# A decoder layer on one core: the queries' scale moved into constants, two Z projections moved into the attention steps, and the last stage's VectorE order written by hand

## The chip, the cores and the metric

The kernel runs on one core of a Trainium2 chip. The core has five engines, each with its own instruction queue that is worked off in order: TensorE (PE, matmuls), VectorE (DVE), ScalarE (ACT), GpSimd (POOL) and SyncE (SP, which here only issues DMA transfers). They meet through semaphores. On-chip data lie in SBUF, results of TensorE in PSUM banks. The metric is the device time of one execution in microseconds; the median over the runs counts.

## The reference

One decoder layer on 1024 tokens of width 1024, in float32, and a last norm:

```python
h = rmsnorm(x, attn_norm_w[l])
proj = h @ w_in[l]
qkv_la, z_la, b_la, a_la, q_d, k_d, v_d = jnp.split(proj, SPLIT_IDX, axis=-1)
qkv_la = jax.nn.silu(causal_conv(qkv_la, conv_w[l]))
...
o_la = gated_delta_rule(q_la, k_la, v_la, g, beta)        # q = l2norm(q) * DK ** -0.5
o_la = rmsnorm(o_la, la_norm_w[l]) * jax.nn.silu(z_la.reshape(B, T, LA_HEADS, LA_DV))
...
o_d = diff_attention(q_d, k_d, v_d, lam, rel_bias)        # p = softmax_0 - lam * softmax_1
o_d = rmsnorm(o_d, diff_norm_w[l], eps=1e-5) * (1.0 - lam_init)
x = x + jnp.concatenate([o_la, o_d], axis=-1) @ w_out[l]
h = rmsnorm(x, ffn_norm_w[l])
gate, up = jnp.split(h @ w_gate_up[l], 2, axis=-1)
x = x + (jax.nn.silu(gate) * up) @ w_down[l]
return rmsnorm(x, final_norm_w)
```

The delta rule and the attention have four heads each (head widths 128). The delta rule's output is normalized per token and head (`rmsnorm`), so a constant factor on its queries matters only against the norm's epsilon.

## The kernel before

**Matmuls.** A float32 product is computed as three products of a reduced type: each operand is split into a high part (a cast) and a low part (the difference), and `mm3` (L147 to L150) adds high x high, high x low and low x high. `split` makes the parts of a weight: the cast on ScalarE (L155), the difference on VectorE (L157, one instruction) or GpSimd (L161, two halves). A projection of one head (`dense_T`, `qk_dense`) is 48 matmuls of 512 columns: 2 halves of the tokens x 8 x 3.

**Stages.** 1. Norm of the input, its transposed high and low parts `xT_h`, `xT_l`, and the convolved projections of the delta rule. 2. The chunks' products: `brk`, `dec`, `At` and the intra-chunk matrix (L513, L516; L520 copies the diagonal blocks), norms of keys and queries by `pow` on GpSimd (`nk` L526, `rqs` L527), and the inverses of the triangular blocks on VectorE (L538 to L545), while TensorE runs the attention's query and key projections of heads 0 and 1 (`qk_dense`; results evacuated by ScalarE at L569 and L570, and stored to DRAM as `qh`, `ql`, `ks`). `TT` (written at L618) holds the transposed inverses. 3. The recurrence over 8 chunks of 128 tokens, whose outputs `Vn` are scaled by `oms` (L739 to L743), and around it the four Z projections (L745 to L749): a `dense_T` each, `Silu` on ScalarE, a store to `sz_dr`. 4. The attention: 32 steps (4 heads x 8 query blocks). A step k has its score matmuls (`emit_S`, L963 and L964), the maximum on VectorE (L969 to L974), the exponentials on ScalarE (L978), the difference of the two maps (`emit_P`, L987 to L990), and, one and two steps later, its transposes (`emit_T`, L1005, copied at L1006) and its values (`emit_PV`, L1020). After every fourth step comes a norm of four blocks (L1027 to L1035, with a `pow` on GpSimd at L1032), and `emit_OT`. 5. The residual, the second norm and the feed-forward network. 6. The last stage: for each row block t the last two rows of the down projection are added (`add`, L1248, two halves), then the final norm (L1555 to L1568) and the output's store.

**Fillers.** TensorE would wait in an attention step for the chain through VectorE and ScalarE. A generator `fill()` (L843) hands out other matmuls: before, the query and key projections of heads 2 and 3, the gate of the delta rule's heads, and the output projection of the delta rule's heads. `pump(n)` takes about n matmuls from it, and `share(k)` (L922) says how many step k takes.

**Pools.** `cv` and `avl` are rotating buffers of four tiles of 128x1024 each: a fifth request waits until the first tile's last reader is done.

**Order.** In stage 4 SyncE's order is that of the code (`manual_schedule`). Everywhere else a scheduler, at build time, sets the order of each engine's queue; so an instruction can stand far ahead of where the code has it. L660 stands in the code after the inverses, in VectorE's queue before them.

Of the kernel before, what the change touches and what calls it, by code (L numbers as in the profile page):

```python
# [8 lines left out]
F32 = mybir.dt.float32  # L9
# [61 lines left out]
def decoder_kernel(ctx: ExitStack, tc: tile.TileContext, a: dict, out: bass.AP):  # L71
# [479 lines left out]
    def qk_dense(h, is_q, ps_of, mid=None):  # L551
        if (h, is_q) not in raws:
            fetch((h, is_q), *qk_col(h, is_q))
        w = take((h, is_q), nc.gpsimd if h > 1 else None)
        yield 0
        sh = cvt(F32R)
        sl = cvt(F32R)
        for n in range(2):
            if n and mid:
                mid()  # L560
            ps = ps_of(n)
            wh, wl = w
            ns = slice(n * 512, (n + 1) * 512)
            for k in range(NK):
                mm3(ps, wh[:, k, :], wl[:, k, :], xT_h[:, k, ns], xT_l[:, k, ns], k == 0, k == NK - 1)
                yield 3
            scale = DH ** -0.5 if is_q else 1.0
            if h < 2:
                nc.scalar.mul(out=sh[:, ns], in_=ps, mul=scale)  # L569
                nc.scalar.mul(out=sl[:, ns].bitcast(F32), in_=ps, mul=scale)  # L570
                if n == 1:
                    nc.vector.tensor_tensor(out=sl, in0=sl.bitcast(F32), in1=sh.bitcast(F32), op=ALU.subtract)
                continue
            nc.scalar.mul(out=sl[:, ns].bitcast(F32), in_=ps, mul=scale)
            nc.scalar.copy(out=sh[:, ns], in_=sl[:, ns].bitcast(F32))
            nc.gpsimd.tensor_tensor(out=sl[:, ns], in0=sl[:, ns].bitcast(F32), in1=sh[:, ns].bitcast(F32),
                                    op=ALU.subtract)
        if is_q:
            nc.scalar.dma_start(out=qh_dr[h], in_=sh.bitcast(F32))
            nc.scalar.dma_start(out=ql_dr[h], in_=sl.bitcast(F32))  # L580
        else:
            nc.scalar.dma_start(out=ks_dr[h].rearrange("(a d) t -> a d t", d=DH)[0::3], in_=sh.bitcast(F32))
            nc.scalar.dma_start(out=ks_dr[h][DH:3 * DH, :], in_=sl.bitcast(F32))
# [69 lines left out]
    for h in range(H):  # L653
        ut = sm()
        for j in range(NT):
# [1 line left out]
                             start=True, stop=True)  # L657
        nc.vector.tensor_scalar(out=TT[h][0:64, :, 64:128], in0=ut[0:64].rearrange("p (j c) -> p j c", c=64),
                                scalar1=-1.0, scalar2=None, op0=ALU.mult)
    nc.vector.tensor_scalar(out=rqs, in0=rqs, scalar1=DK ** -0.5, scalar2=None, op0=ALU.mult)  # L660
    Ktok = gp.tile([P, NHJ, P], F32, name="ak", bufs=1)
    for h in range(H):
        Kh = Ktok[:, h * 8:h * 8 + 8, :]
# [74 lines left out]
    rq = rqs.rearrange(fl)  # L738
    nc.vector.tensor_tensor(out=oms, in0=oms, in1=rq, op=ALU.mult)  # L739
    nc.vector.tensor_tensor(out=oms, in0=oms, in1=rq, op=ALU.mult)  # L740
    nc.vector.tensor_scalar(out=oms, in0=oms, scalar1=1.0 / DV, scalar2=1e-6, op0=ALU.mult, op1=ALU.add)
    nc.gpsimd.tensor_tensor(out=oms, in0=oms, in1=epow_neg, op=ALU.pow)
    nc.vector.tensor_tensor(out=oms, in0=oms, in1=rq, op=ALU.mult)  # L743

    for h in range(H):  # L745
        zps = dense_T(C_Z + h * P, nc.vector)
        sz = cvt()
        nc.scalar.activation(out=sz, in_=zps, func=AF.Silu)
        nc.scalar.dma_start(out=sz_dr[h], in_=sz)  # L749
# [89 lines left out]
    def x2_load(t):  # L839
        x2t[t] = op.tile([P, T], F32, name="avl", bufs=4)  # L840
        nc.sync.dma_start(out=x2t[t], in_=x2_dr[t])

    def fill():  # L843
        one = lambda n: flr()
        yield from qk_dense(2, True, one, lambda: finish_norm(0))
        fetch((3, True), *qk_col(3, True))
        finish_norm(1)
# [74 lines left out]
    def share(k):  # L922
        i = steps[k][1] if k < len(steps) else 0
        prev = steps[k - 1][1] if 0 < k <= len(steps) else 0
        n = 22 - 5 * i / 2
        pb = 4 if prev >= 4 else 0
        return max(0, n - pb - 5), pb, 5

# [129 lines left out]
            nc.scalar.dma_start(out=md[h][:, hc], in_=m)  # L1058

    with tc.manual_schedule(engines={mybir.EngineType.SP}):  # L1060
        fetch((2, True), *qk_col(2, True))
        fetch((2, False), *qk_col(2, False))
        load_head(0)
        load_v(0)
        for k in range(len(steps) + 4):

            def values():
                if 2 <= k < len(steps) + 2:
                    emit_PV(k - 2)

            if k < len(steps):
                emit_S(k, values)
                if k % NT == 0:
                    load_q(k // NT, 1 - first_half(k // NT))
                if k % NT == 4 and k // NT + 1 < H:
                    load_head(k // NT + 1)
                    load_v(k // NT + 1)
            else:
                values()
            if k == 28:  # L1080
                late["mix"][1] = [cvt(F32R) for h in range(H)]
                load_mix_d(1, H - 1)
            pa, pb, pc = share(k)
            pump(pa)
            if 1 <= k <= len(steps):
                emit_T(k - 1, pb)
            pump(pc)
            if k > 2 and (k - 3) % 4 == 3:
                emit_OT(k - 3)
            if k < len(steps):  # L1090
                emit_P(k)
            if k == len(steps):
                while 0 not in late["mix"]:
                    pump(12)
                load_mix_d(0, H - 1)
        while "d1" in late:
            c = next(filler, None)
            if c is None:
                break
# [446 lines left out]
                add(x2[:, i + 4, n0], x2[:, i + 4, n0], mid[:, i, :])  # L1546
                add(x2[:, i + 4, n1], x2[:, i + 4, n1], mid[:, i, :])

    for t in range(NT):
        ssn = small.tile([P, 2], F32, name="ssn", bufs=3)  # L1550
        for n in range(2):
            ns = slice(n * 512, (n + 1) * 512)
            add(x2[:, t, ns], plain(t, n, (NF - 2, NF - 1)), x2[:, t, ns])
            sc = cvt()
            nc.scalar.activation(out=sc[:, ns], in_=x2[:, t, ns], func=AF.Square, accum_out=ssn[:, n:n + 1])  # L1555
        nc.vector.tensor_tensor(out=ssn[:, 0:1], in0=ssn[:, 0:1], in1=ssn[:, 1:2], op=ALU.add)
        nc.vector.tensor_scalar(out=ssn[:, 0:1], in0=ssn[:, 0:1], scalar1=1.0 / D, scalar2=1e-6,
                                op0=ALU.mult, op1=ALU.add)
        nc.gpsimd.tensor_tensor(out=ssn[:, 1:2], in0=ssn[:, 0:1], in1=epow_neg[:, 0:1], op=ALU.pow)
        o = cvt()  # L1560
        for n in range(2):
            ns = slice(n * 512, (n + 1) * 512)
            if n == 0 and t < NT - 1:
                nc.scalar.activation(out=o[:, ns], in_=x2[:, t, ns], func=AF.Copy, scale=ssn[:, 1:2])
                nc.gpsimd.tensor_tensor(out=o[:, ns], in0=o[:, ns], in1=wb3[:, ns], op=ALU.mult)
            else:
                nc.vector.scalar_tensor_tensor(out=o[:, ns], in0=x2[:, t, ns], scalar=ssn[:, 1:2],
                                               in1=wb3[:, ns], op0=ALU.mult, op1=ALU.mult)  # L1568
            nc.sync.dma_start(out=out[0, t * P:(t + 1) * P, ns], in_=o[:, ns])
    close_ep()  # L1570
    late["close_wp2"]()
    late["close_x2"]()
# [32 lines left out]
```

## Time and profile before

| | us |
|---|---|
| runs | 1336.72, 1341.82, 1337.94 |
| median | 1337.94 |
| profiled execution: its own time | 1337.53 |
| its span on the core | 1335.8 |
| TensorE busy | 1267.1 (95%) |
| VectorE busy | 835.5 (63%) |
| ScalarE busy | 530.2 (40%) |
| GpSimd busy | 293.9 (22%) |

The span runs from the first to the last instruction; 1.7 us of the execution's time lie outside it. Busy times are sums over instructions. [...] In a timeline the bracket at a row's end is the engine's idle time before it and what ended it; rows of equal instructions are drawn together (x4).

### The profile page before, as it was taken

The page shows a single profiled execution, that of the slowest core. Times are in us where ns is not written, and L with a number is a line of the kernel's source. Part 1 is how long each engine was busy: PE and PEld are TensorE (multiplying, and loading weights), DVE is VectorE, ACT ScalarE, POOL GpSimd, SP SyncE. Part 2 cuts the span into 40 slices and gives each one's busy share as a digit, 9 for nine tenths or more (in the row PEclk, how much of TensorE's full clock was granted, in tenths as well). Part 3 has the DMA queues.
Part 4 walks back from the last instruction along what each step waited for, and adds up shares of the span by engine and source line. Part 5 has one row for each costly group of instructions (what it writes and reads, how often), then busy time and mean ns, then how long its engine had stood idle before and what let it go on. Part 6 is the DMA issues. An engine that isn't in the chain of part 4 may idle for free.

```text
span 1335.8 us, 17311 instructions
## 1 busy us (share of the span) xinstructions
PE 1267.1 (95%) x6432; PEld 1059.9 (79%) x6432; DVE 835.5 (63%) x1383; ACT 530.2 (40%) x1030; POOL 293.9 (22%) x231
## 2 busy tenths in 40 slices
PE   6999988999999998998979999999999999999996
PEld 6978876798988776887758888888888888778775
DVE  6515756833853776776786556565566536687876
ACT  5224342222544654554553333233323317243314
POOL 1014443200013432113222222212212110121104
PEclk9999998999999998999989999999999999999998
DMA  7425662410026656643512343333323346676503
GB/s 220 115 63 205 221 221 80 136 37 17 18 74 198 200 174 197 229 151 134 177 61 95 119 123 110 106 118 115 113 90 116 103 158 238 204 237 205 188 2 126
DMA packets 143884, 183.44 MB, mean 137 GB/s; under 512 B 15888, under 2 KB 92984, under 8 KB 143800
## 3 DMA queue, kind: packets, MB, share of 16 engines
q1 hardware_dynamic: 135888, 168.19, 39.3%
q10 hardware_dynamic: 7912, 14.16, 2.9%
q8 instruction: 50, 0.82, 0.3%
q14 instruction: 34, 0.28, 0.1%
HBM read 127.00 MB, written 55.32 MB: 136 GB/s over the span
## 4 chain that ended last, share of the span: by engine, by line
PE 62%; DVE 12%; ACT 3%; issue 3%; POOL 3%; DMA 3%; POOLq 0%; DVEq 0%; ACTq 0%
PE big L1236 17%; PE sm L1236 8%; PE big L1535 5%; PE fl L1236 4%; PE fl L1535 3%; PE sm L1535 3%; PE big L148 2%; PE big L149 2%; PE big L150 2%; PE fl L148 2%; PE fl L150 2%; PE fl L149 2%; PE sm L1020 1%; DVE mx L969 1%; DMA ks<-cv 1%
## 5 line engine op out<-in xcount | busy, mean ns | idle before, releaser
L148 PE MATMUL big<-xT_h,w_h 128*128 128x512 f32 x320 | 128.2, 401 | 6.1 <-ACT cv L570 5.7
L150 PE MATMUL big<-xT_h,w_l 128*128 128x512 f32 x320 | 126.8, 397 | 2.0 <-DVE w_l L157 2.0
L149 PE MATMUL big<-xT_l,w_h 128*128 128x512 f32 x320 | 126.5, 395 | 0.0
L1248 DVE TENSOR_TENSOR av<-big,av 128x512 f32<-128x512 f32 x79 | 54.3, 688 | 59.2 <-PE big L1236 59.1
L1236 PE MATMUL big<-hT_h,cv 128*128 128x512 f32 x264 | 85.9, 389 | 0.0
L1236 PE MATMUL big<-hT_h,avl 128*128 128x512 f32 x264 | 85.9, 389 | 0.0
L148 PEld LDWEIGHTS big<-xT_h,w_h 128*128 128x128 f32 x320 | 60.8, 190 | 21.2 <-ACT cv L570 7.6
L150 PEld LDWEIGHTS big<-xT_h,w_l 128*128 128x128 f32 x320 | 60.7, 190 | 15.3 <-DVE w_l L157 2.8
L149 PEld LDWEIGHTS big<-xT_l,w_h 128*128 128x128 f32 x320 | 60.8, 190 | 12.0 <-issue 0.2
L155 ACT CAST w_h<-w_raw 128x1024 fp32r<-128x1024 f32 x32 | 33.5, 1051 | 83.8 <-PE big L149 66.5
L161 POOL TENSOR_TENSOR w_l<-w_raw,w_h 128x512 fp32r<-128x512 f32 x28 | 38.2, 1383 | 117.5 <-ACT w_h L155 116.3
L1141 POOL TENSOR_TENSOR avl<-xh,avl 128x512 fp32r<-128x512 f32 x23 | 33.1, 1440 | 138.2 <-ACT avl L1140 138.2
L454 POOL TENSOR_TENSOR avl<-avl 128x512 f32<-128x512 f32 x36 | 49.1, 1363 | 60.1 <-DMA avl<-in_w_down 25.2
L1236 PE MATMUL sm<-hB_h,avl 128*128 128x512 f32 x176 | 59.3, 399 | 1.1 <-ACT hB_h L1166 1.1
L1141 POOL TENSOR_TENSOR cv<-xh,cv 128x512 fp32r<-128x512 f32 x22 | 30.7, 1396 | 132.6 <-ACT cv L1140 132.6
L978 ACT ACTIVATE ae<-big,mx 128x128 f32<-128x128 f32 (+7 forms) x64 | 47.3, 741 | 27.9 <-DVE mx L969 11.9
L1236 PE MATMUL sm<-hB_h,cv 128*128 128x512 f32 x176 | 57.8, 389 | 0.0
L1236 PEld LDWEIGHTS big<-hT_h,avl 128*128 128x128 f32 x264 | 49.6, 188 | 10.3
L1236 PEld LDWEIGHTS big<-hT_h,cv 128*128 128x128 f32 x264 | 49.6, 188 | 10.3
L157 DVE TENSOR_TENSOR w_l<-w_raw,w_h 128x1024 fp32r<-128x1024 f32 x18 | 23.3, 1295 | 52.7 <-ACT w_h L155 35.8
L1513 POOL TENSOR_TENSOR x<-x,w_raw 128x512 f32<-128x512 f32 x16 | 22.0, 1383 | 155.4 <-DVE x L1248 122.7
L1204 DVE TENSOR_TENSOR xh<-w_raw 128x512 f32<-128x512 f32 x45 | 31.6, 701 | 33.9 <-DMA w_raw<-in_w_gate_up 33.9
(451 smaller groups left out, 3627.2 us busy)
## 6 DMA issues: line engine op xcount, KB each, us to landing
w_raw<-in_w_gate_up SPq DMA_DIRECT2D x44, 512.0 KB, 4.0
w_raw<-in_w_in SPq DMA_DIRECT2D x24, 512.0 KB, 4.7
sum<-av SPq DMA_DIRECT2D x45, 256.0 KB, 3.0
avl<-in_w_down SPq DMA_DIRECT2D x18, 512.0 KB, 5.3
rows<-avl SPq DMA_DIRECT2D x18, 512.0 KB, 2.8
w_raw<-sum SPq DMA_DIRECT2D x11, 512.0 KB, 3.5
xh<-sum SPq DMA_DIRECT2D x21, 256.0 KB, 3.9
av<-sum SPq DMA_DIRECT2D x10, 512.0 KB, 3.7
```

The lines of the kernel that those rows point to most:

```text
L148: nc.tensor.matmul(ps, lhsT=lh, rhs=rh, start=start, stop=False)
L149: nc.tensor.matmul(ps, lhsT=lh, rhs=rl, start=False, stop=False)
L150: nc.tensor.matmul(ps, lhsT=ll, rhs=rh, start=False, stop=stop)
L155: nc.scalar.copy(out=h, in_=raw)
L161: eng.tensor_tensor(out=l[:, c], in0=raw[:, c], in1=h[:, c].bitcast(F32), op=ALU.subtract)
L454: nc.gpsimd.tensor_tensor(out=o, in0=x, in1=y, op=ALU.subtract)
L978: nc.scalar.activation(out=e[:, :n].rearrange("p (b c) -> p b c", b=nb), in_=s[:, :, :w], func=AF.Exp, bias=mx[:, m:m + 1], accum_out=zs[: ...
L1141: eng.tensor_tensor(out=l, in0=raw, in1=h.bitcast(F32), op=ALU.subtract)
L1204: nc.vector.tensor_tensor(out=r, in0=a0, in1=a1, op=alu)
L1236: nc.tensor.matmul(ps, lhsT=x[:, k, :], rhs=y[:, k, :], start=begin and k == 0 and n == 0, stop=k == HALF - 1 and n == 2, skip_group_check ...
L1248: nc.vector.tensor_tensor(out=out, in0=in0, in1=in1, op=ALU.add)
L1535: nc.tensor.matmul(pss[i], lhsT=x[:, g_, ts], rhs=y[:, g_, :], start=begin and g_ == 0 and n_ == 0, stop=g_ == GRP - 1 and n_ == 2, skip_g ...
```

## The change

It has four parts.

1. `rqs`, the reciprocal norms of the delta rule's queries, is no longer multiplied by `DK ** -0.5` (L660). The factor goes into two constants where `oms` is made.
2. In `qk_dense` the low part `sl` comes from the pool of `avl` instead of `cv`, but for the last key projection.
3. The Z projections of heads 2 and 3 leave the loop behind the recurrence and become the first two fillers (`z_dense`), with their weights' low parts on GpSimd instead of VectorE and the `Silu` in two halves. `share` hands out 24.67 - 2.5 i instead of 22 - 2.5 i, and SyncE fetches their weights first.
4. The last stage is cut into `final_sum`, `final_norm` and `final_out`, and VectorE's order there is that of the code.

```diff
-        sl = cvt(F32R)
+        sl = cvt(F32R) if (h, is_q) == (H - 1, False) else opt("avl", F32R)
...
-    nc.vector.tensor_scalar(out=rqs, in0=rqs, scalar1=DK ** -0.5, scalar2=None, op0=ALU.mult)
...
-    nc.vector.tensor_scalar(out=oms, in0=oms, scalar1=1.0 / DV, scalar2=1e-6, op0=ALU.mult, op1=ALU.add)
+    nc.vector.tensor_scalar(out=oms, in0=oms, scalar1=1.0 / (DK * DV), scalar2=1e-6, op0=ALU.mult, op1=ALU.add)
     nc.gpsimd.tensor_tensor(out=oms, in0=oms, in1=epow_neg, op=ALU.pow)
-    nc.vector.tensor_tensor(out=oms, in0=oms, in1=rq, op=ALU.mult)
-
-    for h in range(H):
+    nc.vector.scalar_tensor_tensor(out=oms, in0=oms, scalar=DK ** -0.5, in1=rq, op0=ALU.mult, op1=ALU.mult)
+
+    for h in range(2):
         zps = dense_T(C_Z + h * P, nc.vector)
...
+    def z_dense(h):
+        w = take(("z", h), nc.gpsimd)
+        fetch((2, h == 2), *qk_col(2, h == 2))
+        sz = cvt()
+        for n in range(2):
+            ps = flr()
+            ns = slice(n * 512, (n + 1) * 512)
+            for k in range(NK):
+                mm3(ps, w[0][:, k, :], w[1][:, k, :], xT_h[:, k, ns], xT_l[:, k, ns], k == 0, k == NK - 1)
+                yield 3
+            nc.scalar.activation(out=sz[:, ns], in_=ps, func=AF.Silu)
+        nc.scalar.dma_start(out=sz_dr[h], in_=sz)
...
     def fill():
         one = lambda n: flr()
+        yield from z_dense(2)
+        yield from z_dense(3)
         yield from qk_dense(2, True, one, lambda: finish_norm(0))
...
-        n = 22 - 5 * i / 2
+        n = 24.67 - 5 * i / 2
...
-        fetch((2, True), *qk_col(2, True))
-        fetch((2, False), *qk_col(2, False))
+        for h in (2, 3):
+            fetch(("z", h), w_in_v[:, :, C_Z + h * P:C_Z + (h + 1) * P], [P, NK, P])
...
+    with tc.manual_schedule(engines={mybir.EngineType.DVE}):
+        final_sum(0, 0)
+        final_sum(0, 1)
+        for t in range(NT):
+            if t + 1 < NT:
+                final_sum(t + 1, 0)
+            ssn = final_norm(t)
+            if t + 1 < NT:
+                final_sum(t + 1, 1)
+            final_out(t, ssn)
```

VectorE in stage 2, where L660 stood: one piece of the difference (`ak` are the chunks' products, read from PSUM; `rqs` comes from GpSimd's `pow`).

```order
 L501 TENSOR_SCALAR ssq<-ssq 128x8
 L513 SCALAR_TENSOR_TENSOR ak<-fl,brk,dec 128x128 x4
-L660 TENSOR_SCALAR rqs<-rqs 128x32
 L516 TENSOR_TENSOR dec<-sm,dec 128x512
 L513 SCALAR_TENSOR_TENSOR ak<-fl,brk,dec 128x128 x4
```

The row between the two groups of L513 is gone; all else there keeps its order.

ScalarE at the start of the attention, of the kernel before and then of the change (L978 before and L992 now are the exponentials, L852 the `Silu` of a half Z projection, L1006 and L1020 copies of the transposes).

```order
L978 ACT_TABLE_LOAD
L978 ACTIVATE ae,z<-big,mx 128x128 x2
L574 ACTIVATE cv<-fl 128x512
L575 CAST cv<-cv 128x512
L978 ACTIVATE ae,z<-big,mx 128x256 x2
L1006 COPY apt<-sm 128x128
```

```order
L852 ACTIVATE cv<-fl 128x512
L992 ACT_TABLE_LOAD
L992 ACTIVATE ae,z<-big,mx 128x128 x2
L992 ACTIVATE ae,z<-big,mx 128x256 x2
L1020 COPY apt<-sm 128x128
L852 ACT_TABLE_LOAD
L852 ACTIVATE cv<-fl 128x512
L1036 ACTIVATE aon<-sm,rz 128x128
L853 DMA sz_79<-cv 128x1024
L992 ACT_TABLE_LOAD
L992 ACTIVATE ae,z<-big,mx 128x384 x2
```

Each switch from an exponential to a `Silu` and back has a table load; there are seven in the attention now, and one before.

VectorE in the last stage, one row block of the kernel before and then of the change (L1248 and L1262 are the sums, first half from `fl`, second from `sm`; L1567 and L1590 the products that make the output).

```order
L1248 TENSOR_TENSOR x_9138<-fl,x_9138 128x512
L1556 TENSOR_TENSOR ssn<-ssn 128x1
L1557 TENSOR_SCALAR ssn<-ssn 128x1
L1567 SCALAR_TENSOR_TENSOR cv<-x_9138,ssn,wb_9132 128x512
L1248 TENSOR_TENSOR x_9138<-sm,x_9138 128x512
```

```order
L1262 TENSOR_TENSOR x_9143<-fl,x_9143 128x512
L1576 TENSOR_TENSOR ssn<-ssn 128x1
L1577 TENSOR_SCALAR ssn<-ssn 128x1
L1262 TENSOR_TENSOR x_9143<-sm,x_9143 128x512
L1590 SCALAR_TENSOR_TENSOR cv<-x_9143,ssn,wb_9137 128x512
```

The second sum of the next block now stands between the norm's scalars and the product that waits for GpSimd's `pow`.

Two more things come out of the new order. On GpSimd the last norm but one of the attention (L1032 before, L1046 now) stood behind one of four halves of a weight split and stands ahead of all four. And the dense matmuls (three to a k block) that TensorE has ahead of the second score block, then in each attention step, counted from its queue, are:

| | before | after |
|---|---|---|
| behind the recurrence, up to the attention's first blocks | 128 | 54 |
| steps 0 to 7 | 24, 18, 18, 12, 0, 24, 0, 15 | 5, 21, 21, 15, 15, 21, 4, 8 |
| steps 8 to 15 | 21, 12, 21, 3, 0, 24, 11, 6 | 24, 12, 0, 24, 33, 12, 3, 21 |
| steps 16 to 23 | 7, 0, 24, 36, 12, 9, 9, 9 | 3, 0, 24, 19, 5, 0, 30, 9 |
| steps 24 to 30 | 9, 9, 9, 12, 15, 15, 0 | 9, 12, 12, 15, 15, 21, 21 |
| last reader of `xT` at the end of step | 13 | 18 |

## Rows read from the trace of the kernel before

**Rows 1.** The page, part 1: busy time, share of the span, instructions.

```profile
PE 1267.1 (95%) x6432; PEld 1059.9 (79%) x6432; DVE 835.5 (63%) x1383; ACT 530.2 (40%) x1030; POOL 293.9 (22%) x231
```

**Rows 2.** Windows: stretch, length, busy time by engine, mean clock, DMA share.

```profile
core 0: us, PE busy (x) PEld busy (x) DVE busy (x) ACT busy (x) POOL busy (x), PEclk, DMA share, GB/s
210.00:230.00 20.00, 13.53 (x45) 9.68 (x45) 16.78 (x40) 4.46 (x10) 1.60 (x1) 0.74 0.23 79
414.00:640.00 226.00, 209.37 (x1158) 175.58 (x1157) 156.75 (x284) 121.16 (x273) 63.30 (x51) 0.98 0.55 177
510.00:530.00 20.00, 15.48 (x81) 13.55 (x81) 11.02 (x22) 8.99 (x24) 2.87 (x3) 0.83 0.69 216
610.00:620.00 10.00, 6.19 (x27) 5.19 (x27) 7.49 (x17) 3.26 (x11) 2.46 (x2) 0.83 0.72 243
```

**Rows 3.** Timeline of VectorE, 201 to 212: start, duration, instruction, idle before.

```profile
201.68 1.13 DVE L513 SCALAR_TENSOR_TENSOR ak<-fl,brk,dec 128x128 f32<-128x128 f32 x4
211.64 0.18 DVE L660 TENSOR_SCALAR rqs<-rqs 128x32 f32<-128x32 f32 x1 [8.83 <-POOL rqs L527]
```

**Rows 4.** Timeline of GpSimd, 206 to 212 and 606 to 609.

```profile
206.16 5.44 POOL L527 TENSOR_TENSOR rqs<-ssq,expo 128x32 f32<-128x32 f32 x1
...
606.05 1.29 POOL L161 TENSOR_TENSOR w_l<-w_raw,w_h 128x512 fp32r<-128x512 f32 x1 [7.39 <-ACT w_h L155]
607.30 1.00 POOL L1032 TENSOR_TENSOR ams<-ams,expo 128x4 f32<-128x4 f32 x1
```

**Rows 5.** Timeline of TensorE, 211 to 226 and 247 to 248.

```profile
211.62 0.39 PE L148 MATMUL big<-xT_h,w_h 128*128 128x512 f32 x1
...
212.76 0.39 PE L150 MATMUL big<-xT_h,w_l 128*128 128x512 f32 x1
216.81 0.79 PE L148 MATMUL big<-xT_h,w_h 128*128 128x512 f32 x1 [3.66 <-ACT cv L570]
...
220.06 0.79 PE L150 MATMUL big<-xT_h,w_l 128*128 128x512 f32 x1 [2.03 <-DVE w_l L157]
...
225.63 0.50 PE L148 MATMUL big<-xT_h,w_h 128*128 128x512 f32 x1
...
247.56 0.50 PE L148 MATMUL big<-xT_h,w_h 128*128 128x512 f32 x1 [1.22 <-ACT cv L570]
```

**Rows 6.** Timeline of ScalarE, at four places.

```profile
213.48 1.22 ACT L520 COPY av<-ak 32x128 f32<-32x128 f32 x4 [9.43 <-DVE ak L513]
...
245.49 0.60 ACT L569 ACTIVATE cv<-big 128x512 fp32r<-128x512 f32 x1 [1.83 <-DMA ks<-cv]
...
414.34 1.28 ACT L978 ACT_TABLE_LOAD   x1 [0.44 <-ACT cv L748]
...
514.67 1.04 ACT L155 CAST w_h<-w_raw 128x1024 fp32r<-128x1024 f32 x1 [4.48 <-DMA w_raw<-in_w_out]
```

**Rows 7.** The tile `ks` (keys in DRAM): its transfers.

```profile
DMA to landing us min/median/max: 7.6/10.4/12.9
```

**Rows 8.** Timeline of VectorE in the last stage, 1308 to 1333.

```profile
1308.12 0.75 DVE L1567 SCALAR_TENSOR_TENSOR cv<-x,ssn,wb 128x512 f32<-128x512 f32 x1 [0.73 <-POOL ssn L1559]
...
1311.40 0.75 DVE L1567 SCALAR_TENSOR_TENSOR cv<-x,ssn,wb 128x512 f32<-128x512 f32 x1 [0.73 <-POOL ssn L1559]
...
1328.57 0.68 DVE L1248 TENSOR_TENSOR x<-sm,x 128x512 f32<-128x512 f32 x1
...
1331.20 1.42 DVE L1567 SCALAR_TENSOR_TENSOR cv<-x,ssn,wb 128x512 f32<-128x512 f32 x2 [0.75 <-POOL ssn L1559]
```

**Rows 9.** Timeline of TensorE: its last matmul.

```profile
1323.96 0.39 PE L150 MATMUL sm<-w_h,w_l 128*128 128x512 f32 x1
```

**Rows 10.** Waits of TensorE from 414 to 640: total, times, longest.

```profile
PE big L963 <- ACT ae L978: 6.7, 6, 4.4
PE sm L1005 <- DVE ae L990: 6.5, 5, 3.8
```

**Rows 11.** Timeline of VectorE near 608.

```profile
608.34 1.23 DVE L1033 TENSOR_TENSOR ams<-ams,aok 128x4 f32<-128x4 f32 x1 [2.23 <-POOL ams L1032]
```

More of the change, by code (lines that the diff above doesn't have):

```diff
@@ L1547, in decoder_kernel, with final_sum, final_norm @@
                 add(x2[:, i + 4, n1], x2[:, i + 4, n1], mid[:, i, :])
[L1549 to L1555, printed above, removed]
+    sq = {}
+    def final_sum(t, n):
+        if n == 0:
+            sq[t] = small.tile([P, 2], F32, name="ssn", bufs=3), cvt()
+        ssn, sc = sq[t]
+        ns = slice(n * 512, (n + 1) * 512)
+        add(x2[:, t, ns], plain(t, n, (NF - 2, NF - 1)), x2[:, t, ns])
+        nc.scalar.activation(out=sc[:, ns], in_=x2[:, t, ns], func=AF.Square, accum_out=ssn[:, n:n + 1])
+    def final_norm(t):
+        ssn = sq.pop(t)[0]
         nc.vector.tensor_tensor(out=ssn[:, 0:1], in0=ssn[:, 0:1], in1=ssn[:, 1:2], op=ALU.add)
@@ L1559, in decoder_kernel, with final_out @@
         nc.gpsimd.tensor_tensor(out=ssn[:, 1:2], in0=ssn[:, 0:1], in1=epow_neg[:, 0:1], op=ALU.pow)
+        return ssn
+    def final_out(t, ssn):
         o = cvt()
```

## The prediction

> **What bounds the kernel now.** [...] Four places come out, one for each part of the change. At 212.8 to 225.6 us TensorE stands and then runs at half clock: the mean granted clock of 210 to 230 is 0.74 [rows 2]. At 247.6 it stands 1.22 us [rows 5]. In the attention (414 to 640) it is busy 209.37 of 226 us, so 16.6 us idle, and the mean clock of 0.98 is worth some 4.5 us more (226 x 0.02) [rows 2]. At the end TensorE is done at 1323.96 + 0.39 = 1324.35 [rows 9], while VectorE works until 1331.20 + 1.42 = 1332.62 [rows 8]. At full rate dense matmuls of 512 columns start 0.228 us apart: five spacings from 211.62 to 212.76 [rows 5].
>
> **The queries' scale.** L660 multiplies `rqs`, which comes from a `pow` on GpSimd. VectorE reaches L660 at 202.8 and waits 8.83 us, until GpSimd is through at 206.16 + 5.44 = 211.6 [rows 3, 4]. Its result is needed only at the end of the recurrence. Queued behind it are the rest of the second half's products (L516, L513), so ScalarE's copies of them (L520, which waits 9.43 us, until 213.48 [rows 6]), which stand ahead of the next weight cast (L155) and the evacuations L569/L570. TensorE waits 3.66 us for L570 and 2.03 us for the weights' low part (L157), which is behind the same queue on VectorE [rows 5]. Between 212.76 and 225.63 TensorE issues 12 dense matmuls; at 0.228 us they would be through at 212.99 + 12 x 0.228 = 215.73. What the stall costs, idle time and half clock together, is 225.63 - 215.73 = **9.9 us**. With L660 gone nothing that VectorE has queued there waits for GpSimd (front, first order piece). VectorE is 8.8 us earlier, L520 begins near 205 instead of 213.5, and the cast, evacuations and L157 come to about 211 to 212, just ahead of TensorE's 212.99. Bounds: 5.7 us if only the two long waits go and the clock still falls; 9.9 if all goes. I take 9.9: the low clock is seen only behind the idle time. The two edits at the recurrence's end put a number into another constant and a `tensor_tensor` becomes a `scalar_tensor_tensor` on 128x32: nothing.
>
> **The low parts in the other pool.** ScalarE waits 1.83 us at 245.49 for the store of a head's keys to leave `cv` [rows 6], and TensorE 1.22 us behind it [rows 5]. With `sl` in `avl` that buffer is free: **-1.2 us**. In exchange the four `TT` tiles, which are `avl` too, now wait for these stores before VectorE may write them (L618). A key's store takes 7.6 to 12.9 us to land [rows 7]; behind L618 on VectorE stands the value convolution. Bounds: -1.2 to +3 us (a key's store issued near 245 may land at 258, and VectorE then has to catch up before TensorE runs out of projections); I take -1.2, since the order puts several projections of TensorE between.
>
> **Two Z projections in the attention.** By the table in the section on the change, 128 dense matmuls stand ahead of the attention's second score block before, and 54 now: TensorE comes there 74 x 0.228 = 16.9 us earlier, and has the same 74 more inside and behind the attention. Its work is unchanged; what counts is how much of the 16.6 + 4.5 us of stalls the 74 fill, and what they add. Stall by stall:
> - At 610 TensorE waits 3.8 us for L990 [rows 10]. VectorE stood 2.23 us at L1033 for GpSimd's L1032, which had begun only after a weight split L161 [rows 4, 11], and step 30 held no fillers. Now L1046 (the old L1032) is ahead of all four splits, and step 30 holds 21 fillers: the stall goes, with the lower clock behind it (0.83 in 610 to 620 [rows 2], 1.7 us): -5.5.
> - At 513 it waits 4.4 us for the exponentials [rows 10], which stand on ScalarE behind a cast that waits 4.48 us for an output weight [rows 6]; with the clock of 0.83 in 510 to 530, worth 20 x 0.17 = 3.4 us [rows 2], 7.8 us. These weights can be fetched only when the last reader of `xT` is done, which by the table now falls at the end of step 18 instead of 13. Behind it step 19 asks for output fillers at once, and steps 20 and 21 hold 5 and 0. The weights come as slowly as before, so I expect this stall again, smaller, since step 19's first 11 fillers need only the one weight that is fetched ahead: 5 us for 7.8, so -2.8.
> - The other 8.4 us of idle time are pieces up to 1.5 us. Most steps get three fillers more (share 22 to 24.67), but steps 0, 6, 14, 16, 17, 20 and 21 get 0 to 5: I leave them equal.
> - The half-width `Silu`s alternate with exponentials: seven table loads of ScalarE instead of one (second order piece). One costs 1.28 us and 0.44 before it [rows 6]. ScalarE has room (121 of 226 us busy [rows 2]); five stand ahead of an instruction that waits for TensorE or VectorE anyway; one waits for the maximum itself: +1.3.
>
> Sum **-7.0 us**. Bounds: -15 if nearly all stalls go, +5 if a step with few fillers stalls as step 17 did and nothing else improves. The Z weights' low parts go from VectorE to GpSimd (1.29 us a piece [rows 4]), where they are done before the first attention normalization.
>
> [...]
>
> **The last stage.** A row block takes VectorE 1311.40 - 1308.12 = 3.28 us, of which 0.73 is a wait for GpSimd's `pow`, with the next block's sums queued behind [rows 8]; TensorE needs 12 x 0.228 = 2.74 us for the block. So VectorE falls behind, and the last sum begins at 1328.57, 4.2 us after the last matmul. In the new order (third order piece) a sum fills the wait: 3.28 - 0.73 = 2.55 us, under 2.74, so the last sum follows the last matmul at 1324.4. From it to the last product's end it is as before 1332.62 - 1328.57 = 4.05 us, hence 1328.45 instead of 1332.62. Bounds -2.5 (half the lag stays) to -4.2; I take **-4.0**.
>
> **Sum.** The profiled execution took 1337.53 us, 0.4 under the median of the runs, 1337.94. 1337.53 - 9.9 - 1.2 - 7.0 - 4.0 = 1315.4 us.
>
> **Rivals.**
> - *The attention's stalls only move.* Each step is longer by its Z matmuls, and the changeover costs as before: 1322.4. For it: both big stalls come from a late helper (an output weight, GpSimd), and fillers do not make those earlier. Against: the order takes GpSimd's wait away.
> - *The table loads are on the path*, 6 x (1.28 + 0.44) = 10.3 us: 1325.7. For it: they are in the first steps, where chains are short. Against: 15 to 21 fillers, 3.4 to 4.8 us, in each of steps 1 to 5. [...]
> - *VectorE stands at another place*: L618 waits for key stores, or the clock stays low near 215. Then the first two parts give 5.7 - 3 = 2.7 instead of 11.1 us: 1323.8.
> - *Nearly all stalls go*, -15 instead of -7: 1307.4. For it: at 0.228 us the 56 matmuls within the steps are 12.8 us, most of the idle time. Against: a stall needs them in its own step.
> - *Slower: the second head pair's keys.* Head 2's keys are stored near step 12 now and read at step 16. A step is 226/32 = 7.1 us, so four steps are 28 us; the store lands in 7.6 to 12.9 [rows 7], and a load behind it takes SyncE's queue. TensorE stands at step 16 for what is over 28 us, and it must be 22.1 us over to undo the sum, three steps' delay: 1338 and more.
>
> **How the numbers follow.** My forecast (1311 to 1319) has 0.42, stalls that move 0.22, table loads 0.08, another wait of VectorE 0.10, nearly all stalls gone 0.14, the late keys 0.02, and 0.02 for no gain because small losses meet. The range 1304 to 1328 leaves out the last two, and the tail of the table loads. A difference under 0.5% (6.7 us) can't be told from none here: faster means under 1331.3, and takes every case but the last two and a tail of the second and third: 0.94; same 0.04; slower 0.02.
>
> **What would show it.** Right: VectorE's L513 groups 0.2 us apart near 203, TensorE without a gap from 205 to 245 and a granted clock of 1.00 in 210 to 230; no idle time of ScalarE for a key store; TensorE's waits in the attention near 10 us instead of 16, the largest at the changeover near step 18; seven table loads with no TensorE wait behind them beyond 1.3 us; a last block whose first product begins within 3 us of the last matmul. Wrong: a VectorE wait for a DMA at L618; more than 5 us of TensorE's waits for exponentials in the first six steps; a low clock anywhere that it was not before; or a TensorE wait at a score matmul for a key load.

## The result, and the profile after

Over five runs each, the changed kernel has a median of 1321.88 us (1315.76 to 1327.25), the kernel before 1336.87 (1336.52 to 1341.82): a ratio of 0.9887, 95% interval 0.9864 to 0.991. It is 15.0 us faster, where 22.1 were predicted, and its runs lie further apart than those of before. The profiled execution took 1327.25 us, the longest of the five; a second profile, of 1322.64 us, is used beside it below (run `after_again`).

The page of the changed kernel, part 1, which answers to [rows 1]: nearly the same busy times in a span 10 us shorter.

```profile
PE 1268.9 (96%) x6432; PEld 1064.5 (80%) x6432; DVE 836.6 (63%) x1380; ACT 537.1 (41%) x1038; POOL 299.4 (23%) x235
```

Windows of the changed kernel, to set beside [rows 2] (the stretch of the attention begins earlier now):

```profile
core 0: us, PE busy (x) PEld busy (x) DVE busy (x) ACT busy (x) POOL busy (x), PEclk, DMA share, GB/s
210.00:230.00 20.00, 19.56 (x86) 15.69 (x86) 18.82 (x42) 4.21 (x7) 1.64 (x1) 1.00 0.42 139
270.00:290.00 20.00, 20.00 (x152) 18.30 (x152) 5.99 (x12) 3.63 (x7) 0.00 (x0) 0.74 0.10 27
396.00:640.00 244.00, 227.47 (x1255) 191.50 (x1254) 158.36 (x289) 134.35 (x288) 67.81 (x56) 0.98 0.56 177
510.00:530.00 20.00, 13.96 (x62) 11.38 (x62) 10.84 (x20) 11.06 (x25) 5.01 (x4) 0.83 0.65 224
```

PEclk is the mean clock granted to TensorE. In windows of 1 us it reads 1.00 (full clock here) or 0.50 (half clock), and a value between only where it changes: of 1325 windows 1293 and 24 in the kernel before, 1284 and 30 in the changed one. From 210 to 230 TensorE is busy 19.56 of 20 us and its clock is 1.00: the first stall is gone. From 270 to 290 the mean is 0.74 (0.50 from 272 to 281), though TensorE is busy all 20 us; that is new. The attention idles 16.5 us and has a clock of 0.98, as before.

The six largest waits of TensorE in the changed kernel, 396 to 640, which answer to [rows 10]: total, times, longest.

```profile
PE fl L148 <- DVE cv L803: 3.8, 2, 3.0
PE sm L1034 <- ACT apt L1020: 3.6, 1, 3.6
PE sm L1019 <- ACT apt L1020: 2.4, 2, 1.9
PE fl L148 <- DVE avl L828: 2.3, 3, 1.6
PE big L977 <- ACT ae L992: 1.8, 3, 0.8
PE sm L1019 <- DVE ae L1004: 1.1, 1, 1.1
```

The waits for L990 (now L1004), of which one of 3.8 us stood behind GpSimd, are down from 6.5 us in all to 1.1 [rows 10]. In their place are 3.8 us for L803, the delta rule's gate. In the kernel before (414 to 640) the same line was L804, and it cost

```profile
PE fl L148 <- DVE cv L804: 1.1, 2, 0.8
```

A table by stage shows where the time went. The marks are the starts of the last product of the chunks (L510 before), the first small matmul of the inverses (L629), the first transpose of the keys (L667), the first transpose of the second norm (L1152), the last one of those, the end of the last matmul, and the end of VectorE's queue; the times are differences in us.

| from, to | before | after | after_again | only_scale | all_but_z | only_z | only_last |
|---|---|---|---|---|---|---|---|
| chunk products, inverses | 70.25 | 59.59 | 59.57 | 60.25 | 59.59 | 70.90 | 70.64 |
| inverses, key transposes | 32.04 | 36.67 | 32.05 | 32.05 | 32.05 | 32.05 | 32.05 |
| key transposes, second norm | 334.54 | 332.46 | 332.76 | 335.79 | 334.58 | 333.73 | 334.85 |
| second norm | 42.33 | 42.10 | 40.84 | 42.31 | 42.31 | 41.12 | 42.32 |
| to the last matmul's end | 641.88 | 641.57 | 640.26 | 640.68 | 640.70 | 639.18 | 640.36 |
| last matmul, end | 11.39 | 10.22 | 10.26 | 11.38 | 9.97 | 11.37 | 10.40 |

The first row holds the first two parts, the third and fourth row the Z projections, the last row the last stage. Up to the first mark the profiles differ by up to 4 us among themselves (201.1 to 205.2), in stages that the change does not touch, so totals of single profiles are not compared.

### The profile page after: what moved, and what is told of

The parts are those of the page before. It is cut to its first block, busy times and chain, and to the rows that moved or that the text cites. A ratio compares the mean times of both kernels' runs of the same rounds, so it can differ in the third digit from the quotient of the medians.

```text
span 1325.5 us, 17315 instructions
## 1 busy us (share of the span) xinstructions
PE 1268.9 (96%) x6432; PEld 1064.5 (80%) x6432; DVE 836.6 (63%) x1380; ACT 537.1 (41%) x1038; POOL 299.4 (23%) x235
## 4 chain that ended last, share of the span: by engine, by line
PE 43%; DVE 5%; issue 1%; ACT 1%; DMA 1%; POOL 1%; POOLq 0%; DVEq 0%; ACTq 0%
PE big L1250 17%; PE sm L1250 8%; PE big L1549 5%; PE fl L1250 4%; PE fl L1549 3%; PE sm L1549 3%; DVE ebl L1265 1%; DMA w_raw<-in_w_gate_up 1%; DVE xh L1218 1%; PE fl L148 0%; PE fl L150 0%; PE fl L149 0%; DVE x L1262 0%; DVE av L1262 0%; DVE cv L1590 0%
## 5 line engine op out<-in xcount | busy, mean ns | idle before, releaser
L148 PE MATMUL big<-xT_h,w_h 128*128 128x512 f32 x288 | 115.6, 401 | 0.9 <-DVE ssk L500 0.5
L149 PE MATMUL big<-xT_l,w_h 128*128 128x512 f32 x288 | 113.9, 395 | 0.0
L150 PE MATMUL big<-xT_h,w_l 128*128 128x512 f32 x288 | 113.8, 396 | 0.0
L1262 DVE TENSOR_TENSOR av<-big,av 128x512 f32<-128x512 f32 x79 | 54.3, 688 | 59.5 <-PE big L1250 59.4
L161 POOL TENSOR_TENSOR w_l<-w_raw,w_h 128x512 fp32r<-128x512 f32 x32 | 42.2, 1342 | 194.8 <-ACT w_h L155 194.8
L148 PEld LDWEIGHTS big<-xT_h,w_h 128*128 128x128 f32 x288 | 54.6, 190 | 14.1 <-issue 2.0
L150 PEld LDWEIGHTS big<-xT_h,w_l 128*128 128x128 f32 x288 | 54.4, 189 | 11.2 <-issue 0.2
L149 PEld LDWEIGHTS big<-xT_l,w_h 128*128 128x128 f32 x288 | 54.6, 190 | 10.7 <-issue 0.2
L1250 PEld LDWEIGHTS big<-hT_h,cv 128*128 128x128 f32 x264 | 49.6, 188 | 10.2
L992 ACT ACTIVATE ae<-big,mx 128x128 f32<-128x128 f32 (+7 forms) x64 | 47.1, 739 | 23.7 <-DVE mx L983 15.7
```

Of the source, the lines that this page charges most:

```text
L148: nc.tensor.matmul(ps, lhsT=lh, rhs=rh, start=start, stop=False)
L149: nc.tensor.matmul(ps, lhsT=lh, rhs=rl, start=False, stop=False)
L150: nc.tensor.matmul(ps, lhsT=ll, rhs=rh, start=False, stop=stop)
L161: eng.tensor_tensor(out=l[:, c], in0=raw[:, c], in1=h[:, c].bitcast(F32), op=ALU.subtract)
L992: nc.scalar.activation(out=e[:, :n].rearrange("p (b c) -> p b c", b=nb), in_=s[:, :, :w], func=AF.Exp, bias=mx[:, m:m + 1], accum_out=zs[: ...
L1250: nc.tensor.matmul(ps, lhsT=x[:, k, :], rhs=y[:, k, :], start=begin and k == 0 and n == 0, stop=k == HALF - 1 and n == 2, skip_group_check ...
```

## The experiments

Each ran beside the kernel before on the same chip. "Before" is that kernel's median there.

**only_scale**: the kernel before with the first part.

```diff
-    nc.vector.tensor_scalar(out=rqs, in0=rqs, scalar1=DK ** -0.5, scalar2=None, op0=ALU.mult)
...
-    nc.vector.tensor_tensor(out=oms, in0=oms, in1=rq, op=ALU.mult)
+    nc.vector.scalar_tensor_tensor(out=oms, in0=oms, scalar=DK ** -0.5, in1=rq, op0=ALU.mult, op1=ALU.mult)
```

> The kernel before with the first part alone (no multiplication of rqs, the factor in the two constants). My theory: VectorE's 8.8 us wait for GpSimd was the whole cause of the stall near 213, so the time falls by 9 to 10 us, to about 1327.5, and the granted clock of 210 to 230 is 1.00; the 1.2 us wait for the key store near 237 stays. Rival, the small matmuls: the profile of the change shows half clock from 271 to 281 with no idle time before it, and if that comes from this part, the gain is 5 us (about 1332) and the low clock stands in this profile too. Second rival, the wait only moves: VectorE meets the next wait, gain under 6 us with TensorE waits for L570 and L157 still there.

Measured 1326.99 us (before 1336.93; ratio 0.9926, 0.9909 to 0.9942): 9.9 us. The first stage of the table is 10.0 us shorter, the clock of 210 to 230 is 1.00, and there is no low clock near 271 in its profile. My theory holds. Both rivals fall by the time, since they would have given 5 us and under 6. That the low clock is absent from one profile says little, since it comes in some executions only (after_again).

**only_last**: the kernel before with the last stage's hand-written order.

```diff
-    for t in range(NT):
...
+    with tc.manual_schedule(engines={mybir.EngineType.DVE}):
```

> The kernel before with the last part alone (the last stage's VectorE order). My theory after the result: the first scalar of the norm, a VectorE instruction with two SBUF operands, now falls into GpSimd's product of 1.3 us and is held until that ends (0.75 instead of 0.15 us), so a block takes 3.06 us instead of 2.55 and VectorE still falls behind: gain 1.9 us, about 1335.5, too little to be told by the medians, but the profile shows 6.4 us from the last matmul's end to the last VectorE instruction's end instead of 8.3. Rival, my prediction's term: 4.0 us, about 1333.5, with 4.1 us between the two ends.

Measured 1335.33 us (before 1336.93; ratio 0.9989, 0.9976 to 1.0003). From the last matmul's end to the end of VectorE's last product it is 1329.30 + 1.42 - 1323.87 = 6.85 us, against 8.27 before ([rows 8, 9]) and 1320.67 + 1.41 - 1315.27 = 6.81 in the changed kernel: 1.4 us gained, nearer to the 1.9 than to the 4.0. The interval of the ratio includes 1, so the medians can't tell this from no gain, and the profile decides here. Its timeline of VectorE shows the stretched sum, L1561:

```profile
1317.13 0.75 DVE L1575 SCALAR_TENSOR_TENSOR cv<-x,ssn,wb 128x512 f32<-128x512 f32 x1 [0.16 <-POOL ssn L1564]
1317.80 0.68 DVE L1248 TENSOR_TENSOR x<-fl,x 128x512 f32<-128x512 f32 x1
1318.50 0.75 DVE L1561 TENSOR_TENSOR ssn<-ssn 128x1 f32<-128x1 f32 x1
1319.28 0.15 DVE L1562 TENSOR_SCALAR ssn<-ssn 128x1 f32<-128x1 f32 x1
1319.35 0.68 DVE L1248 TENSOR_TENSOR x<-sm,x 128x512 f32<-128x512 f32 x1
```

**only_z**: the kernel before with the third part (`z_dense`, the share of 24.67, SyncE's fetches, as in the change).

```diff
-    for h in range(H):
+    for h in range(2):
         zps = dense_T(C_Z + h * P, nc.vector)
...
+        yield from z_dense(2)
+        yield from z_dense(3)
```

> The kernel before with the third part alone (two Z projections as fillers, the new share, SyncE's new fetches). My theory after the result: 2.5 to 4 us, about 1334, since the stalls mostly move (a changeover stall of 3 to 4 us in step 18 or 19 with half clock behind it, one of 2 to 3 us behind the delta rule's gate), while the one behind GpSimd at step 30 goes. Rival, my prediction's term: 7 us, about 1330. Rival, the stalls only move: 0, about 1337.

Measured 1334.42 us (before 1336.93; ratio 0.9985, 0.9975 to 0.9996), 1331.3 to 1337.9 over ten runs: 2.5 us. The longest wait is not the gate's but one of 4.3 us, for a copy (L1021) that stands on ScalarE behind a cast waiting for the keys' store to leave `cv`:

```profile
481.30 0.62 ACT L575 CAST cv<-cv 128x512 fp32r<-128x512 f32 x1 [4.91 <-DMA ks<-cv]
481.82 0.58 ACT L1021 COPY apt<-sm 128x512 f32<-128x512 f32 x1
```

So alone, without the second part, the third runs into a wait that the second takes away. The size fits the theory.

**all_but_z**: the changed kernel without the third part.

```diff
-        yield from z_dense(2)
-        yield from z_dense(3)
...
-        n = 24.67 - 5 * i / 2
+        n = 22 - 5 * i / 2
```

> The changed kernel without the third part (all four Z projections behind the recurrence again, the old share). My theory: the first, second and last part give 10.7 and 1.9 us, so about 1324.5 when the clock stays up near 271, and some 5 us more when it falls there. Rival: if half clock near 271 belongs to the Z part's changed order, this kernel never shows it. Rival for the Z part: if it is worth its 7 us, this kernel is 7 us slower than the changed kernel in runs without the low clock, 1322.5; if it is worth 3.6, 1319.

Measured 1323.93 us (before 1336.93; ratio 0.9907, 0.9892 to 0.9921), and only 1323.55 to 1324.63 over its runs. The Z part is worth 1323.93 - 1321.88 = 2.05 us in the medians. These come from different rounds, and the changed kernel's runs spread over 11 us, so the figure is no firmer than only_z's 2.5. The two rivals for the Z part (7 and 3.6 us) don't fit. The clock near 271 is 1.00 here, which one profile can't settle.

**after_again**: the changed kernel, unchanged.

> The changed kernel once more, for a second profile. Its five runs lay between 1315.8 and 1327.3, and the profiled one was the slowest, with a mean granted clock of 0.986. Theory A: the half clock of 271 to 281, which falls without idle time among small matmuls, comes in some executions only; a profile of a faster execution has the clock at 1.00 there and the rest as before, and the time is about 5 us shorter. Theory B: the low clock near 271 is in every execution, and the spread comes from the attention.

Measured 1321.73 us (before 1337.56; ratio 0.9877, 0.9851 to 0.9903), 1319.07 to 1328.84. The profile (1322.64 us) has the clock at 1.00 from 265 to 285, and the second row of the table is 32.05 instead of 36.67: theory A as to the low clock:

```profile
265.00:285.00 20.00, 20.00 (x191) 19.05 (x191) 9.50 (x15) 7.60 (x12) 2.50 (x2) 1.00 0.11 28
```

It is not the whole spread: the second norm's stage also differs, by 1.3 us.

**sl_in_cv**: the changed kernel without the second part.

```diff
-        sl = cvt(F32R) if (h, is_q) == (H - 1, False) else opt("avl", F32R)
+        sl = cvt(F32R)
```

> The changed kernel with the second part undone (low parts in the pool of convolution tiles again); TensorE's order is the same as in the changed kernel. My theory: two ScalarE waits for key stores come back, the one near 237 (1.2 us of TensorE) and, in the attention, one of 4 to 5 us in front of a cast, which the profile of the Z part alone showed (4.3 us of TensorE and half clock behind it): 5 to 7 us slower than the changed kernel, about 1327. Rival, by the first one alone: 1.2 us, about 1323. Second rival: VectorE's wait for a key store at L618 (8.3 us) costs by leading to the low clock near 271; without it the clock there is 1.00 and the time is not longer.

Measured 1321.61 us (before 1337.56; ratio 0.9881, 0.9852 to 0.991): no difference from the changed kernel, so my theory of 5 to 7 us falls. Its first stage is 60.22 us, 0.65 longer than after_again's 59.57, so the second part gains half of what I gave it. In the attention the wait of 4.3 us for the copy does come, but the gate's wait of 3.0 is down to 0.9 in return: the stage takes 333.32 us against 332.76.

**fused_norm**: the changed kernel with one instruction where the last norm had two.

```diff
-                             func=AF.Square, accum_out=ssn[:, n:n + 1])
+                             func=AF.Square, scale=D ** -0.5, accum_out=ssn[:, n:n + 1])
...
-        nc.vector.tensor_tensor(out=ssn[:, 0:1], in0=ssn[:, 0:1], in1=ssn[:, 1:2], op=ALU.add)
-        nc.vector.tensor_scalar(out=ssn[:, 0:1], in0=ssn[:, 0:1], scalar1=1.0 / D, scalar2=1e-6,
-                                op0=ALU.mult, op1=ALU.add)
+        nc.vector.tensor_scalar(out=ssn[:, 0:1], in0=ssn[:, 0:1], scalar1=ssn[:, 1:2], scalar2=1e-6,
+                                op0=ALU.add, op1=ALU.add)
```

> The changed kernel with the two scalars of the last norm in one VectorE instruction: ScalarE's squares are scaled by 1/32 before they are summed, and a tensor_scalar adds the second sum, as a pointer operand, and the epsilon. My theory: the instruction has one tensor operand, is not held by GpSimd's product as the two-operand sum was (0.75 instead of 0.15 us), a block takes under the matmuls' 2.72 us, and the end comes 2.2 us earlier: 4.1 us instead of 6.4 from the last matmul's end to the last VectorE instruction's. Rival: the wait is for something else in the order (GpSimd's pow comes late by its own product of 1.3 us before it), so the block stays at about 3 us.

Measured 1322.59 us (before 1337.56; ratio 0.9877, 0.985 to 0.9904); the spread of the medians hides an effect of 2 us. The profile shows it: the timeline of VectorE in the last stage,

```profile
1306.48 0.69 DVE L1262 TENSOR_TENSOR x<-sm,x 128x512 f32<-128x512 f32 x1 [0.55 <-PE sm L150]
1307.09 0.74 DVE L1589 SCALAR_TENSOR_TENSOR cv<-x,ssn,wb 128x512 f32<-128x512 f32 x1
1307.84 0.69 DVE L1262 TENSOR_TENSOR x<-fl,x 128x512 f32<-128x512 f32 x1
1308.44 0.20 DVE L1576 TENSOR_SCALAR ssn<-ssn 128x1 f32<-128x1 f32 x1
1309.20 0.69 DVE L1262 TENSOR_TENSOR x<-sm,x 128x512 f32<-128x512 f32 x1 [0.55 <-PE sm L150]
```

A block takes 1309.20 - 1306.48 = 2.72 us, and VectorE waits for the matmuls now, not they for it. The 0.20 us of L1576 lie inside GpSimd's product, which runs from 1307.61 to 1308.99:

```profile
1307.61 1.38 POOL L1587 TENSOR_TENSOR cv<-cv,wb 128x512 f32<-128x512 f32 x1 [0.84 <-ACT cv L1586]
```

From the last matmul's end to the end of the queue it is 7.67 us against 10.26, 3.7 less than the kernel before's 11.39. My theory holds.

**head_later7**: the changed kernel with SyncE's loads of head 2 three steps later.

```diff
-                if k % NT == 4 and k // NT + 1 < H:
+                if k % NT == (7 if k // NT == 1 else 4) and k // NT + 1 < H:
```

> The changed kernel with SyncE's loads of head 2 (queries, keys, bias, values) three steps later, behind the third gate's load and an output weight; no other engine's order changes. My theory: SyncE stood until 473 for the store of head 2's keys, and the load for the delta rule's gate came behind it, which held VectorE at L803 for 3.75 us and TensorE for 2.97 at 481. With the gate's load first that wait goes, 3 us less, about 1319 in the median, and head 2's loads, now near 480, are still there for step 16. Rival: the loads come too late and TensorE waits for them at the first score matmuls of head 2, 2 to 5 us, so nothing is gained. Second rival: the gate's load lands as late as before, since the transfer queues are busy with the weights.

Measured 1318.04 us (before 1337.56; ratio 0.986, 0.983 to 0.9889), with runs between 1315.47 and 1325.63. In the changed kernel SyncE's queue read

```profile
450.42 1.23 SPq L778 DMA_DIRECT2D aql<-ql  x2
473.18 0.38 SPq L760 DMA_DIRECT2D ak<-ks  x1
...
475.49 0.39 SPq L797 DMA_DIRECT2D cv<-sz  x1
```

21.5 us in front of the keys' load, with the gate's load (L797) behind it, and VectorE then stood at the gate:

```profile
483.12 0.75 DVE L803 SCALAR_TENSOR_TENSOR cv<-fl,rim,cv 128x512 f32<-128x512 f32 x1 [3.75 <-DMA cv<-sz]
```

With the gate's load ahead that row of VectorE is

```profile
472.90 0.74 DVE L803 SCALAR_TENSOR_TENSOR cv<-fl,rim,cv 128x512 f32<-128x512 f32 x1
```

without a wait, head 2's loads cause none, and the stage up to the second norm takes 327.36 us. Profiles of one order differ there by some 2 us: with the early load it is 332.46, 332.76 and (fused_norm) 334.65, with the late one 327.36 and (best) 329.65, so about 5 us. Over these five profiles TensorE's idle time in the stage is 16.3, 17.7 and 16.6 us with the early load, 12.9 and 15.1 with the late one, and half clock lasts 10.2, 6.8 and 13.7 us against 6.8 and 6.8. On average that is 2.9 us less idle time, the size of the gate's wait, and 1.7 us less lost to the clock. My theory holds as to the wait; the size is less sure, since the medians give 1321.73 - 1318.04 = 3.7 us and runs of one kernel spread over 10.

**best**: fused_norm and head_later7 together.

> The changed kernel with both repairs: SyncE's later loads of head 2 and the last norm's scalars in one instruction. My theory: the two are in different stages and add up, 3.5 to 5 us and 2.2 to 2.5 us: 1315 to 1316 in the median, against 1318.0 and 1322.6 with either alone. Rival: the gain of the later loads was chance between executions (its profile was also 4 us ahead by 273, before any change of it can act), and the median stays at 1318 or more.

Measured 1313.35 us (1312.22 to 1313.91; before 1337.57; ratio 0.9821, 0.9806 to 0.9836): 24.2 us less than the kernel before and the fastest of all. The end takes 7.65 us. It is 1321.9 - 1313.4 = 8.5 us less than the changed kernel, of which the stages show about 5 and 2.6. The medians of either repair alone (3.7 us less and 0.9 us more than after_again) don't add up to it. Part of the 8.5 us may be chance: none of best's four runs has a mean granted clock under 0.992, while two of head_later7's six have 0.986 and are its slowest (1323.53 and 1325.63 us).

**late_cast**: best, with the second half's output weights asked for later.

```diff
-        w.append(take_o(0, 1, nc.gpsimd))
-        fetch_o(1, 0, 0)
-        fetch_o(1, 0, 1)
...
+            if n == 3:
+                w.append(take_o(0, 1, nc.gpsimd))
+                fetch_o(1, 0, 0)
+                fetch_o(1, 0, 1)
```

> The kernel of both repairs with one more: the split of the second half's output weights, and the fetches behind it, are asked for after the third output unit instead of before the first. My theory: the largest stall that is left, 3.4 us at the changeover, comes from a copy of transposes that stands on ScalarE behind a cast waiting for an output weight; with the copy ahead of the cast it goes, and the half clock behind it: 3 to 6 us less, 1310 to 1313. Rival: TensorE then waits for the weights themselves, or for a cast one step later, and the time is the same or longer.

Measured 1318.78 us (before 1337.57; ratio 0.9858, 0.9838 to 0.9877): slower than best. Its waits of TensorE in the attention begin with

```profile
PE fl L148 <- DVE xh L828: 4.2, 1, 4.2
PE sm L1020 <- ACT apt L1021: 3.2, 2, 2.8
PE sm L1020 <- DVE ae L1005: 2.2, 1, 2.2
```

The 3.6 us behind the cast are gone and 4.2 for an output unit's sum (L828) stand in their place, much as the rival says. Its profile also has the low clock near 271 (0.74 in 270 to 290), worth 4.7 us by the inverses' stage (36.71 us). The stage of the attention takes 331.15 us, against 329.65 in best and 327.36 in head_later7, so how much of the loss is the edit's stays open; a gain it is not.

**z_copy**: the changed kernel without the six table loads (and without the `Silu` of heads 2 and 3).

```diff
-            nc.scalar.activation(out=sz[:, ns], in_=ps, func=AF.Silu)
+            nc.scalar.copy(out=sz[:, ns], in_=ps)
```

> The changed kernel with a plain copy instead of the Silu of the two moved Z projections (so the gates of heads 2 and 3 lack their Silu), which takes six table loads out of ScalarE; a weight cast moves ahead of one pair of exponentials with it. My theory: the loads lay beside other work, and the first score step to the feed-forward network takes as long as in the changed kernel, within 1.5 us. Rival, the table loads are on the path: 8 to 10 us less in the attention, about 1312.

Measured 1323.84 us (before 1337.57; ratio 0.9903, 0.9878 to 0.9928). The stage takes 335.15 us against 332.46 and 332.76: not shorter, so the rival's 8 to 10 us fall. An effect of 1 or 2 us would be hidden, since fused_norm, with the changed kernel's order here, takes 334.65. It is longer by more than the 1.5 us that I allowed, with a wait of 3.1 us in place of 1.9 among the largest; the change in ScalarE's order that came with the edit may be the reason, which was not tried.

## Why the prediction was right in direction and too large

**The queries' scale: right.** The term was 9.9 us; the median gave 9.9 and the stage 10.0 with this part alone.

**The low parts: half.** The term was 1.2 us; the stages give 60.25 - 59.59 = 0.66 and, with the part undone, 0.65. With the scale's wait gone, TensorE waits there only 0.9 us in two pieces (only_scale), so there was less to win. In the medians nothing shows (sl_in_cv, 1321.61 against 1321.73). The wait that I feared came, and cost nothing in this stage. The timeline of VectorE in the changed kernel:

```profile
259.62 1.23 DVE L618 TENSOR_TENSOR avl<-av,mats 128x1024 f32<-128x1024 f32 x1 [8.33 <-DMA ks<-avl]
```

**The Z projections: the stalls moved, and their sum did not shrink.** The term was 7.0 us; the medians give 2.1 to 2.5, the stages 334.54 - 332.46 = 2.1 and, in the second norm's, 0.2 to 1.5 more. The step that failed is the list "stall by stall". Its first line was right: the stall behind GpSimd at step 30 is gone. The second, a changeover stall of 5 us, was too small: 3.56 us of idle time and 20 x 0.17 = 3.4 of clock, hardly less than the 7.8 of before (in after_again 3.96 and, at a clock of 0.91, 1.8). And the line "I leave them equal" missed a new stall, SyncE's queue behind head 2's keys, which delays the gate's load. I had named that wait as the slower rival, but priced it at the scores of step 16, where the keys are read, and not at what is queued behind the load on SyncE. Taking it away gave about 5 us by the stage, so I estimate the part at about 7 with this queue in another order; no run has that order without the part.

The forecast was that moved matmuls fill stalls, and in sum they did not: TensorE idles 16.5 us in the attention, against 16.6 before. The 2.1 us lie elsewhere. From the first key transpose to the first score matmul it is 89.6 us instead of 106.4, from there to the second norm 242.9 (after_again 243.2) instead of 228.2. So the 74 moved matmuls, 16.9 us at full rate, made the attention only about 15 us longer; what took up the other 2 is not shown. The prediction's 56 matmuls within the steps are 50 by its own table (11.4 us), which changes no term.

The table loads cost little, as forecast: z_copy, without six of them, was not faster (335.15 us of the stage against 332.46). No run shows a load dearer than the prediction's 1.28 + 0.44 us, as its tail above 1328 us would need. The 0.44 us that the prediction added to each load was ScalarE's issue of a store (L749, 0.33 us at 413.93), no part of the switch. The second load of a pair stands 0.00 us behind the `Silu` before it:

```profile
404.93 0.60 ACT L852 ACTIVATE cv<-fl 128x512 f32<-128x512 f32 x1
405.53 1.28 ACT L992 ACT_TABLE_LOAD   x1
406.82 0.69 ACT L992 ACTIVATE ae<-big,mx 128x512 f32<-128x512 f32 x1
```

From one function's end to the next's start it is 406.82 - 405.53 = 1.29 us. The load fills 1.28 us of them.

**The last stage: a term mis-sized.** It was 4.0 us, and 1.0 to 1.4 came at the end of the program. The step that failed is "3.28 - 0.73 = 2.55 us": it took every row's duration from the old order. In the new one the sum of the two halves (L1556 before, 0.15 to 0.16 us in all eight blocks; L1576 now, up to 0.75, the median 0.73) falls into GpSimd's product. The timelines of VectorE and, below, of GpSimd in the changed kernel, which answer to [rows 8]:

```profile
1308.51 0.75 DVE L1590 SCALAR_TENSOR_TENSOR cv<-x,ssn,wb 128x512 f32<-128x512 f32 x1 [0.16 <-POOL ssn L1579]
1309.18 0.69 DVE L1262 TENSOR_TENSOR x<-fl,x 128x512 f32<-128x512 f32 x1
1309.88 0.75 DVE L1576 TENSOR_TENSOR ssn<-ssn 128x1 f32<-128x1 f32 x1
1310.66 0.15 DVE L1577 TENSOR_SCALAR ssn<-ssn 128x1 f32<-128x1 f32 x1
...
1311.57 0.75 DVE L1590 SCALAR_TENSOR_TENSOR cv<-x,ssn,wb 128x512 f32<-128x512 f32 x1 [0.16 <-POOL ssn L1579]
```

```profile
1309.32 1.30 POOL L1588 TENSOR_TENSOR cv<-cv,wb 128x512 f32<-128x512 f32 x1 [0.84 <-ACT cv L1587]
```

The sum ends at 1310.63, GpSimd's product at 1310.62; a block takes 1311.57 - 1308.51 = 3.06 us, over the matmuls' 2.72. In the kernel before the sum began at 1310.32, when the product (1308.92 + 1.30 = 1310.22) was through:

```profile
1310.32 0.16 DVE L1556 TENSOR_TENSOR ssn<-ssn 128x1 f32<-128x1 f32 x1 [0.25 <-ACT cv L1555]
```

```profile
1308.92 1.30 POOL L1565 TENSOR_TENSOR cv<-cv,wb 128x512 f32<-128x512 f32 x1 [0.84 <-ACT cv L1564]
```

In fused_norm the instruction in the same place has one tensor input and takes 0.20 us inside the product. Why the sum of two inputs lasts until the product's end is not shown. With that repair the term is 11.39 - 7.67 = 3.7 us.

**The sum.** 10.0 + 0.7 + 2.1 + 1.2 by the stages, and 0.2 to 1.5 in the second norm's, is 14.2 to 15.5; the medians give 15.0. The low clock near 271, 4.6 us of the profiled execution, is not in this sum.

The time is inside the predicted range, 2.9 us above the forecast's own 1311 to 1319, and within 0.5 us of the rival "the attention's stalls only move" (1322.4). As to the stalls that rival was right. That its number fits so well is luck: it has nothing for the Z part and 4.0 us for the last stage, where the runs gave 2.1 or more and 1.2. Two signs that the prediction had named for being wrong came, VectorE's wait for a DMA at L618 and a low clock where there was none, and TensorE's waits in the attention stayed near 16 us instead of 10.

With both repairs 24.2 were measured, where 22.1 were predicted for the change alone.

## What to carry to other kernels

Before a load is moved to where its data are younger, read what stands behind it in the same DMA queue: the price of its wait can be that of the next load's user, not of its own (here 3.75 us of VectorE at L803). When an order is rewritten, an instruction's duration may change with its new neighbour (here a VectorE sum from 0.16 to 0.75 us beside GpSimd's product), so check small sums against what GpSimd runs beside them. An instruction that is not needed until much later can still cost most of all where a scheduler lets it wait at the head of a queue (here L660, 9.9 us).

## What the runs showed of the hardware

In the first profile of the changed kernel the granted clock fell without idle time near it. TensorE's only gap from 205 to 300 us is one of 0.44 us that ends at 226.4. From 262.5 it worked through seven groups of 16 narrow matmuls (64 or 32 columns) back to back, and came out of them at half clock (1.00 in each us up to 271, 0.61 in the next, then 0.50 up to 281):

```profile
271.54 1.97 PE L643 MATMUL sm<-avl,av 128*64 128x64 f32 x16
273.44 3.62 PE L641 MATMUL fl<-av,avl 128*128 128x32 f32 x16
276.87 0.78 PE L148 MATMUL big<-xT_h,w_h 128*128 128x512 f32 x1
```

The same groups, in the same order, ran at full clock (1.00 in 270 to 300) in the profiles of the kernel before and of ten other runs (one of them the changed kernel again), and at half clock in the one of late_cast (0.55 in 270 to 280); it cost 4.6 and 4.7 us (36.67 and 36.71 us of a stage that takes 32.05). What decides between the two stays open. I had tied a low clock to idle time alone.
